# Layer 0 of a hybrid decoder step: full-size products for two small transposes, one place for a head's sample reads, and one set of four places for all merges

## The chip, the cores and the metric

The kernel runs on one core of one Trainium2 chip. The metric is the device time of one execution in microseconds: 2222.28 us is the median of three runs (2222.04 to 2224.26). A core has five engines that work side by side, each through its own instructions in order: TensorE (PE in the profile, with its weight loads as PEld), VectorE (DVE), ScalarE (ACT), GpSimd (POOL) and SyncE (SP), which here issues all DMA transfers. They wait for each other through semaphores.

## The reference: what is computed

A two-layer decoder trunk is run on a prompt of 16 + 1024 tokens and on 8 sample sequences of 8 tokens each: 1104 token columns in all, float32 throughout. Layer 0 is a gated DeltaNet, layer 1 an RWKV-7 mixer. Only layer 0 is touched by the change:

```
proj = xn @ w_in                                  # q, k, v, z, b, a
qkv, new_buf = causal_conv(qkv, conv_buf, conv_w) # width 4; new_buf = last 3 rows
L = where(strict, (k*beta) k^T * decay, 0);  A = L + I
u, wk = A^-1 [v*beta, k*beta*exp(gc)]             # unit lower triangular
step: v_new = u - wk S;  o = q_dec S + attn v_new;  S = S*exp(gl) + k_dec^T v_new
```

The causal convolution needs, for each of the 8 samples, the three rows before its first token (24 rows of history for each 128 channels), and it returns the last three rows of each of the 8 samples and of the prompt (27 rows). The triangular inverse is made of 32-row blocks: these are inverted one by one and then merged to 64 and to 128 rows. The samples' tokens read the samples' own states.

## The kernel before

**Tiling.** The 1104 columns are cut into three segments of 384, 384 and 336. A dense projection tile is 128 output channels by one segment: 24 products (8 contraction tiles, each as high x high, low x high and high x low part in a 32-bit reduced form) that add up in one PSUM buffer. In the trace these are `dq`, `dk`, `dv`, `dz`.

**Order.** Layer 0 issues its instructions in exactly the order in which they are written. `dense_gaps` emits a dense tile and calls `L.gap()` after each 6 products; this is a *gap*, and the gaps are numbered. All other work is put into the numbered gaps with `L.put(gap, function, priority)` or `L.steps`; within one gap a smaller priority comes first. A pair of value heads (j = 0 to 7) owns 72 gaps from `B = base(j) = 24 + 72 j`. So each engine's queue is a fixed sequence: an instruction that waits holds up everything behind it on its engine.

**Convolution (`conv_plan`).** For each of 32 channel tiles: `load` brings the history, 24 rows by 128 channels, from memory; `head` turns it with a PE transpose (line 607) into PSUM, from where DVE copies it into the row buffer `raw`; `out` copies a dense result into `raw`; `first` starts the taps and copies the last tokens' columns into `last` on POOL (lines 628 and 630); `ending` turns `last` (128 channels by 27 columns) with a PE transpose (line 652); `store` writes it. `hist` and `last` have two buffers each. The arithmetic helpers are `transpose` (line 126) and `mm` (line 129), so the profile shows these two lines for nearly all of PE's work.

**Preparation (`prep_plan`).** It makes the decay-weighted blocks `E`, sends their 32-row diagonal blocks through memory into `invA`, inverts them in 31 elementwise steps (lines 690 and 692; on POOL for j = 1 to 6, on DVE for j = 0 and 7), and then, in the gaps i0+1 to i0+7 after the last step's gap i0, stores the result and brings it back in two arrangements: ACT copies a turned form (line 815), which goes to memory as `g_u` (gap i0+3); `T1n` is loaded in gap i0+4 (3 transfers); `TT` for segment 0, 1 and 2 is loaded in gaps i0+5, i0+6 and i0+7 (4 transfers each), from `g_u`. SP issues them in that order, with the weight loads (`wraw`), the history loads and others in between. i0 is B+48 for j = 1 to 6.

**Merges.** `merge(s)` merges segment s in eight steps: products Y of 32 rows, their copies by DVE, products U of 32 rows (which need `TT` of segment s), their copies by ACT and DVE, Y of 64 rows, a copy, U of 64 rows, a copy. Two steps go in one gap. Segment 0 has the gaps i0+8 to i0+11, segment 1 i0+9 to i0+12, segment 2 i0+12 to i0+15. The PSUM buffers are `u` (one buffer) for segments 0 and 2, and `f` (two buffers) for segment 1. The products use only a 32x32 or 64x64 part of PE's array. A product of float32 operands shows as two records.

**Sample reads (`sample_read_plan`).** Per value head, eight products of 128 x 32 stationary columns (line 929, `usr` in the trace): four in one gap, four in the next.

**Recurrence (`recur_plan`).** Token groups of 128 follow each other every 8 gaps; their products are `rA` in the trace. They run between the same dense products.

Of the kernel before, what the change touches and what calls it, by code (L numbers as in the profile page):

```python
# [88 lines left out]
class Builder:  # L89
# [8 lines left out]
    def t(self, pool, shape, tag, bufs=1, dt=F32):  # L98
        self.uid += 1
        return pool.tile(shape, dt, name=f"{tag}_{self.uid}", tag=tag, bufs=bufs)  # L100
# [485 lines left out]
    def conv_plan(self, ends, ft, dst, done=None):  # L586

        nc, i, t, L, fp = self.nc, self.i, self.t, self.line, self.fp
        c = Ctx()
        f = slice(128 * ft, 128 * ft + 128)  # L590
        cw = [self.cw[:, k, ft:ft + 1] for k in range(4)]
        raws, ys = [], []
        wd = lambda s: SEGS[s][1] + (24 if s == 0 else 0)
        prev = lambda s: raws[s][:, wd(s):wd(s) + 3]
        v11 = lambda x: x[:, 0:88].rearrange("p (b r) -> p b r", r=11)
        v8 = lambda x: x.rearrange("p (b r) -> p b r", r=8)
        v3 = lambda x: x.rearrange("p (b r) -> p b r", r=3)

        def load():
            c.hist = t(fp, [24, 128], "hist", 2)  # L600
            nc.sync.dma_start(c.hist, i["state_gdn_conv"][0].rearrange("b r c -> (b r) c")[:, f])

        def head():
            x = t(fp, [128, 411], "raw", 3)
            raws.append(x)
            hp = self.ps("f", 2, "hist")
            self.transpose(hp[:, 0:24], c.hist)
            nc.vector.tensor_copy(v11(x)[:, :, 0:3], v3(hp[:, 0:24]))
            nc.gpsimd.memset(x[:, 88:91], 0.0)

        def out(s, p):
            n = SEGS[s][1]
            if s == 0:
                x = raws[0]
                nc.scalar.copy(v11(x)[:, :, 3:11], v8(p[:, 0:64]))
                nc.scalar.copy(x[:, 91:411], p[:, 64:384])
            else:
                x = t(fp, [128, 411], "raw", 3)
                raws.append(x)
                nc.gpsimd.tensor_copy(x[:, 0:3], prev(s - 1))  # L620
                nc.scalar.copy(x[:, 3:3 + n], p[:, 0:n])

        def first(s):
            ys.append(t(fp, [128, 408], "cvy", 2))
            self.act(ys[s][:, 0:wd(s)], raws[s][:, 0:wd(s)], AF.Identity, scale=cw[0])
            if s == 0:
                c.last = t(fp, [128, 27], "last", 2)
                nc.gpsimd.tensor_copy(v3(c.last[:, 0:24]), v11(raws[0])[:, :, 8:11])
            elif s == 2:
                nc.gpsimd.tensor_copy(c.last[:, 24:27], prev(2))  # L630

        def tap(s, *ks):
            for k in ks:
                nc.vector.scalar_tensor_tensor(ys[s][:, 0:wd(s)], raws[s][:, k:k + wd(s)], cw[k], ys[s][:, 0:wd(s)], op0=ALU.mult, op1=ALU.add)  # L634

        def tanh(s):
            self.act(raws[s][:, 0:wd(s)], ys[s][:, 0:wd(s)], AF.Tanh, scale=0.5)

        def silu(s):
            e, y, d, n = raws[s], ys[s], dst(s), SEGS[s][1]  # L640
            one = lambda d, e, y: nc.vector.scalar_tensor_tensor(d, e, 1.0, y, op0=ALU.add, op1=ALU.mult)
            if s == 0:
                one(v8(d[:, 0:64]), v11(e)[:, :, 0:8], v11(y)[:, :, 0:8])
                one(d[:, 64:384], e[:, 88:408], y[:, 88:408])
            else:
                one(d[:, 0:n], e[:, 0:n], y[:, 0:n])
                if n < 384:
                    nc.vector.memset(d[:, n:384], 0.0)

        def ending():  # L650
            lp = self.ps("f", 2, "last")
            self.transpose(lp[0:27, 0:128], c.last)
            c.ls = t(fp, [27, 128], "lasts", 1)
            nc.vector.tensor_copy(c.ls, lp[0:27, 0:128])

        def store():
            nc.sync.dma_start(self.o["s_gdn_conv"][0].rearrange("b r c -> (b r) c")[:, f], c.ls[0:24])
            nc.sync.dma_start(self.o["p_gdn_conv"][0, 0][:, f], c.ls[24:27])

        L.put(ends[0] - 11, load, 2)  # L660
        L.put(ends[0] - 2, head, 2)
        for s, e in enumerate(ends):
            L.put(e + 1, lambda s=s: first(s), 1.5)
            L.put(e + 2, lambda s=s: tap(s, 1, 2), 2)
            L.put(e + 3, lambda s=s: tap(s, 3), 2)
            L.put(e + 4, lambda s=s: tanh(s), 2)
            L.put(e + 5, lambda s=s: silu(s), 1.7)
            if done is not None:
                L.put(e + 8, lambda s=s: done(s), 2.2)
        L.put(ends[2] + 5, ending, 2.5)  # L670
        L.put(ends[2] + 8, store, 3)
        return out

# [28 lines left out]
    def gdn_front(self, right):  # L702
        self.fp = right.enter_context(self.tc.tile_pool(name="gfront", bufs=1, side="right", reuse_waits="tile"))
        self.T1n = None

    def gdn_zero(self):
        self.T1n = self.t(self.fp, [128, 18, 64], "T1n")
        self.nc.gpsimd.memset(self.T1n, 0.0)

        self.kqm = self.t(self.fp, [128, 4, 4, 32], "kqm")  # L710
        self.nc.gpsimd.memset(self.kqm, 0.0)
# [20 lines left out]
    def prep_plan(self, j, B, G, o, pace):  # L732

        nc, t, fp, col, L = self.nc, self.t, self.fp, self.col, self.line
# [97 lines left out]
        i0 = B + 15 + o + int(30 * pace)  # L832
        L.steps(i0, inv, range(1, 8), 1.4)

        v = lambda p, k: p[:, 0:6 * k].rearrange("p (c i) -> p c i", i=k)
        half = lambda s: (("u", 1), ("f", 2), ("u", 1))[s]

        def merge(s):
            LT, TT, T1 = G.E[s].rearrange("p t h k -> p (t h) k"), G.TT[s], self.T1n
# [28 lines left out]
            for q in range(6):  # L868
                self.mm(v(p, 64)[0:64, q], Ys[64:128, q], TT[64:128, q, 64:128])
            self.act(TT[0:64, :, 64:128], v(p, 64)[0:64], AF.Identity, scale=-1.0)  # L870
        for s, at in enumerate((0, 1, 4)):
            m = merge(s)
            for u in range(4):
                L.put(i0 + 8 + at + u, lambda m=m: next(m, None), 1)
                L.put(i0 + 8 + at + u, lambda m=m: next(m, None), 1.05)

    def values_done(self, G, h, s):
        nc = self.nc
# [29 lines left out]
    def sample_read_plan(self, j, B, G):  # L908

        nc, t, L = self.nc, self.t, self.line  # L910
        Sb, c = {}, Ctx()

        def load(h, g):
            x = Sb[h, g] = t(self.gp, [128, 4, 128], "Sb", 3)
            nc.sync.dma_start(x, self.i["state_gdn"][0, 4 * g:4 * g + 4, 2 * j + h].rearrange("b k v -> k b v"))

        def spread():
            kqm = self.kqm.rearrange("p b x (c r) -> p (b x c) r", r=8)
            for x, z in ((0, G.K[0]), (1, G.Q[0])):
                for g in (0, 1):  # L920
                    a = 8 * x + 4 * g
                    nc.gpsimd.tensor_copy(kqm[:, a:a + 52:17], z[:, 32 * g:32 * g + 32].rearrange("p (b r) -> p b r", r=8))

        def mults(h, bs):
            if h == 0 and bs[0] == 0:
                c.ps = self.ps("u", 1, "sr")
            for b in bs:
                for q in range(4):
                    self.mm(c.ps[32 * q:32 * q + 32, 128 * h:128 * h + 128], self.kqm[:, b, q], Sb[h, q % 2][:, b], b == 0, b == 3)

        def out():
            S = G.sS = t(self.gp, [64, 2, 256], "sS", 1)
            for x in (0, 1):
                nc.scalar.copy(S[:, x], c.ps[64 * x:64 * x + 64, 0:256])
        for g, x in ((12, (0, 0)), (14, (0, 1)), (15, (1, 0)), (22, (1, 1))):
            L.put(B + g, lambda x=x: load(*x), 3)
        L.put(B + 14, spread, 2.6)
        for g, x in ((18, (0, (0, 1))), (19, (0, (2, 3))), (26, (1, (0, 1))), (27, (1, (2, 3)))):
            L.put(B + g, lambda x=x: mults(*x), 2.5)
        L.put(B + 28, out, 2.5)  # L940

# [1690 lines left out]
```

## Time and profile before

| | |
|---|---|
| runs | 2222.28 us median of 3 (2222.04 to 2224.26) |
| the profiled execution | span 2227.4 us, 5.1 us above the runs' median |
| PE busy | 2142.1 us, 96% of the span |
| DVE, ACT, POOL busy | 1411.3, 1265.0, 1237.8 us (63, 57, 56%) |
| one group of 72 gaps of layer 0 (268.8 to 389.0) | 120.2 us, PE busy 119.2 us, POOL busy 85.4 us |
| mean granted TensorE clock | 0.977 |

The gap work of layer 0 can be followed in the trace by tile names: `fhist`, `flast`, `usr`, and `uY`, `fY`, `uU`, `fU` for the merges' products. In a timeline a row gives the start, the time from the start of its first to the end of its last instruction, the engine, the line, the operation and its tiles, and the number of instructions that follow each other; a bracket gives the idle time ahead and what ended it. The ends of pipelined products are modelled, so costs are best read from starts: the time from one dense product's start to another's, less the usual step of the dense products in between, is the price of what was put there.

### The profile page before, as it was taken

The page shows a single profiled execution, that of the slowest core. Times are in us where ns is not written, and L with a number is a line of the kernel's source. Part 1 is how long each engine was busy: PE and PEld are TensorE (multiplying, and loading weights), DVE is VectorE, ACT ScalarE, POOL GpSimd, SP SyncE. Part 2 cuts the span into 40 slices and gives each one's busy share as a digit, 9 for nine tenths or more (in the row PEclk, how much of TensorE's full clock was granted, in tenths as well). Part 3 has the DMA queues.
Part 4 walks back from the last instruction along what each step waited for, and adds up shares of the span by engine and source line. Part 5 has one row for each costly group of instructions (what it writes and reads, how often), then busy time and mean ns, then how long its engine had stood idle before and what let it go on. Part 6 is the DMA issues. An engine that isn't in the chain of part 4 may idle for free.

```text
span 2227.4 us, 55333 instructions
## 1 busy us (share of the span) xinstructions
PE 2142.1 (96%) x20382; PEld 1977.4 (89%) x20382; DVE 1411.3 (63%) x3638; ACT 1265.0 (57%) x3651; POOL 1237.8 (56%) x1890
## 2 busy tenths in 40 slices
PE   8989999999999999989999999999999999999997
PEld 7879989899999989978999999998988977888886
DVE  7858575766757585975435762667546347667764
ACT  6526565556655565645433464756546466667663
POOL 3418678585858585525241442227768646666663
PEclk9999999999999999999999999999999999999997
DMA  4324242424243333435254235587885566656532
GB/s 120 84 59 133 66 123 73 114 80 115 79 115 96 101 107 76 132 78 171 91 151 105 69 102 172 180 256 199 229 242 147 160 187 166 171 150 177 160 115 88
DMA packets 495400, 291.61 MB, mean 131 GB/s; under 512 B 222345, under 2 KB 480506, under 8 KB 495130
## 3 DMA queue, kind: packets, MB, share of 16 engines
q1 hardware_dynamic: 495130, 288.08, 46.1%
q8 instruction: 161, 2.64, 0.5%
q14 instruction: 109, 0.89, 0.1%
HBM read 195.66 MB, written 92.30 MB: 129 GB/s over the span
## 4 chain that ended last, share of the span: by engine, by line
PE 68%; DVE 13%; POOL 6%; DMA 5%; ACT 4%; issue 3%; SPq 1%; DVEq 0%; POOLq 0%; ACTq 0%
PE d L129 14%; PE dz L129 7%; PE dv L129 7%; PE rA L133 6%; PE rA L129 5%; PE zo L129 3%; PE do L129 3%; PE dk L129 3%; DVE cvy L634 2%; POOL invT L692 2%; PE fG L129 2%; POOL invtmp L690 2%; PE dq L129 2%; DMA wraw<-in_gdn_w_out 1%; DVE invT L692 1%
## 5 line engine op out<-in xcount | busy, mean ns | idle before, releaser
L143 POOL TENSOR_TENSOR wlo<-wraw,whi 128x512 fp32r<-128x512 f32 x190 | 251.4, 1324 | 229.5 <-ACT whi L139 207.2
L692 POOL TENSOR_TENSOR invT<-invT,invtmp 72x31 f32<-72x31 f32 (+36 forms) x341 | 213.4, 626 | 26.7
L634 DVE SCALAR_TENSOR_TENSOR cvy<-raw,cw,cvy 128x408 f32<-128x408 f32 (+2 forms) x288 | 203.4, 706 | 29.7 <-ACT cvy L115 25.7
L690 POOL TENSOR_TENSOR invtmp<-invA,invT 72x31 f32<-72x31 f32 (+36 forms) x341 | 202.6, 594 | 20.4 <-POOL invT L678 0.8
L129 PE MATMUL d<-xc,whi 128*128 128x384 f32 (+1 forms) x640 | 180.8, 344 | 1.0 <-ACT whi L139 0.8
L139 ACT CAST whi<-wraw 128x512 fp32r<-128x512 f32 x238 | 145.7, 614 | 27.6 <-DMA wraw<-in_rwkv_w_rkvz 13.9
L129 PE MATMUL dv<-xc,whi 128*128 128x384 f32 (+1 forms) x480 | 154.5, 343 | 0.0
L129 PE MATMUL dz<-xc,whi 128*128 128x384 f32 (+1 forms) x480 | 153.0, 342 | 0.0
L115 ACT ACTIVATE w<-rA,nbp 128x128 f32<-128x128 f32 x144 | 45.2, 364 | 152.3 <-PE rA L129 149.9
L129 PEld LDWEIGHTS d<-xc,whi 128*128 128x128 f32 x640 | 118.6, 192 | 3.5 <-ACT whi L139 1.1
L129 PE MATMUL d<-xc,wlo 128*128 128x384 f32 (+1 forms) x320 | 105.5, 339 | 1.9 <-DVE wlo L143 1.9
L160 POOL TENSOR_TENSOR ors<-ovar,cvals 128x6 f32<-128x6 f32 x24 | 34.1, 1422 | 124.6 <-DVE ovar L1122 124.6
L129 PE MATMUL dz<-xa,whi 128*128 128x384 f32 (+1 forms) x288 | 102.6, 356 | 0.5 <-DVE zg L906 0.5
L129 PE MATMUL dv<-xa,whi 128*128 128x384 f32 (+1 forms) x288 | 102.5, 356 | 0.0
L129 PE MATMUL d<-xa,whi 128*128 128x384 f32 (+1 forms) x336 | 100.1, 341 | 1.3 <-ACT whi L139 0.8
L1930 POOL TENSOR_SCALAR y<-y,mv,grs 128x64 f32<-128x64 f32 x132 | 81.7, 640 | 33.1 <-DVE grs L164 27.8
L129 PEld LDWEIGHTS dv<-xc,whi 128*128 128x128 f32 x480 | 89.3, 188 | 3.5 <-issue 3.0
L959 POOL TENSOR_SCALAR Sb<-Sb,eglb 128x128 f32<-128x128 f32 x128 | 88.8, 706 | 5.9 <-DVE usc L752 2.2
L129 PEld LDWEIGHTS dz<-xc,whi 128*128 128x128 f32 x480 | 90.4, 191 | 0.7 <-issue 0.2
L129 PE MATMUL d<-xh,whi 128*128 128x384 f32 (+1 forms) x256 | 82.3, 334 | 0.0
L129 PE MATMUL d<-xl,whi 128*128 128x384 f32 (+1 forms) x256 | 82.3, 335 | 0.0
L129 PE MATMUL d<-xh,wlo 128*128 128x384 f32 (+1 forms) x256 | 82.1, 334 | 0.0
(544 smaller groups left out, 7232.1 us busy)
## 6 DMA issues: line engine op xcount, KB each, us to landing
wraw<-in_gdn_w_in SPq DMA_DIRECT2D x96, 256.0 KB
wraw<-in_rwkv_w_rkvz SPq DMA_DIRECT2D x74, 256.0 KB
Sb<-in_state_gdn SPq DMA_DIRECT2D x64, 256.0 KB
wraw<-in_rwkv_w_o SPq DMA_DIRECT2D x48, 256.0 KB
E<-drow SPq DMA_DIRECT2D x24, 384.0 KB
attn<-drow SPq DMA_DIRECT2D x24, 384.0 KB
wraw<-in_gdn_w_out SPq DMA_DIRECT2D x36, 256.0 KB
out_s_gdn<-Sb SPq DMA_DIRECT2D x32, 256.0 KB
```

The costliest lines, as they stand in the source:

```text
L115: return self.nc.scalar.activation(out, in_, func, bias=bias, scale=scale, **kw)
L129: self.nc.tensor.matmul(out, lhsT, rhs, start=start, stop=stop)
L133: self.nc.tensor.matmul(out, lhsT, rhs, start=start, stop=True, skip_group_check=True)
L139: nc.scalar.copy(hi, x)
L143: e.tensor_tensor(lo, x, hi.bitcast(F32), op=ALU.subtract)
L160: self.nc.gpsimd.tensor_tensor(y, x, half.broadcast_to(sh), op=ALU.pow)
L634: nc.vector.scalar_tensor_tensor(ys[s][:, 0:wd(s)], raws[s][:, k:k + wd(s)], cw[k], ys[s][:, 0:wd(s)], op0=ALU.mult, op1=ALU.add)
L690: v.tensor_tensor(tmp, A[:, j, j + 1:32].unsqueeze(2).broadcast_to([nb, n, m]), Tv[:, j, 0:m].unsqueeze(1).broadcast_to([nb, n, m]), op=AL ...
L692: v.tensor_tensor(Tv[:, j + 1:32, 0:m], Tv[:, j + 1:32, 0:m], tmp, op=ALU.subtract)
L959: nc.gpsimd.tensor_scalar(Sb[g][:, u], Sb[g][:, u], self.eglb[:, hv, 4 * g + u:4 * g + u + 1], None, op0=ALU.mult)
L1930: nc.gpsimd.tensor_scalar(y[:, q], y[:, q], mv[:, q, 0:1], P.rs[:, q:q + 1], op0=ALU.subtract, op1=ALU.mult)
```

## The change

1. `hist` and `last` become one cleared buffer of 128 x 128 each, made once (`cleared`, with a POOL memset; `gdn_front` is called twice). The history's transpose becomes a full product of `hist` with the first 24 columns of the identity, the last tokens' transpose a full product of `last` with the identity. Rows or columns beyond the 24 or 27 are zero. A full product of float32 shows as two records where the transpose showed as one.
2. `ending` moves from gap e+5 at priority 2.5 to gap e+4 at priority 1.4 (e is the last segment's gap).
3. The merges of all three segments are put into the same four gaps, i0+7, i0+9, i0+11 and i0+13, two steps of each segment in each; segment 2 takes the buffers `f` in place of `u`.
4. A head's eight sample reads are put into one gap, the later of the two.

```diff
         def load():
-            c.hist = t(fp, [24, 128], "hist", 2)
-            nc.sync.dma_start(c.hist, i["state_gdn_conv"][0].rearrange("b r c -> (b r) c")[:, f])
+            c.hist = self.hist
+            nc.sync.dma_start(c.hist[0:24], i["state_gdn_conv"][0].rearrange("b r c -> (b r) c")[:, f])
...
             hp = self.ps("f", 2, "hist")
-            self.transpose(hp[:, 0:24], c.hist)
+            self.mm(hp[:, 0:24], c.hist, self.ident[:, 0:24])
...
             if s == 0:
-                c.last = t(fp, [128, 27], "last", 2)
+                c.last = self.last
...
             lp = self.ps("f", 2, "last")
-            self.transpose(lp[0:27, 0:128], c.last)
+            self.mm(lp[:, 0:128], c.last, self.ident)
...
-        L.put(ends[2] + 5, ending, 2.5)
+        L.put(ends[2] + 4, ending, 1.4)
...
     def gdn_front(self, right):
...
         self.T1n = None
+        self.hist = self.cleared("hist")
+
+    def cleared(self, tag):
+        x = self.t(self.fp, [128, 128], tag)
+        self.nc.gpsimd.memset(x, 0.0)
+        return x
 
     def gdn_zero(self):
+        self.last = self.cleared("last")
...
-        half = lambda s: (("u", 1), ("f", 2), ("u", 1))[s]
+        half = lambda s: (("u", 1), ("f", 2), ("f", 2))[s]
...
-        for s, at in enumerate((0, 1, 4)):
+        for s in range(3):
             m = merge(s)
             for u in range(4):
-                L.put(i0 + 8 + at + u, lambda m=m: next(m, None), 1)
-                L.put(i0 + 8 + at + u, lambda m=m: next(m, None), 1.05)
+                L.put(i0 + 7 + 2 * u, lambda m=m: next(m, None), 1)
+                L.put(i0 + 7 + 2 * u, lambda m=m: next(m, None), 1.05)
...
-        for g, x in ((18, (0, (0, 1))), (19, (0, (2, 3))), (26, (1, (0, 1))), (27, (1, (2, 3)))):
+        for g, x in ((19, (0, (0, 1, 2, 3))), (27, (1, (0, 1, 2, 3)))):
             L.put(B + g, lambda x=x: mults(*x), 2.5)
```

## The prediction

> **What bounds the kernel now.** I read first the page's span and busy times, then the busy times of one group of 72 gaps, then who waited for whom on PE in layer 0, and last the timelines around each operation that changes.
>
> ```profile
> span 2227.4 us, 55333 instructions
> PE 2142.1 (96%) x20382; PEld 1977.4 (89%) x20382; DVE 1411.3 (63%) x3638; ACT 1265.0 (57%) x3651; POOL 1237.8 (56%) x1890
> ```
>
> ```profile
> 268.80:389.00 120.20, 119.20 (x1028) 111.29 (x1027) 81.40 (x222) 72.21 (x233) 85.43 (x140) 1.00 0.37 98
> ```
>
> ```profile
> PE usc L129 <- DVE E L766: 3.7, 6, 0.6
> ...
> PE fU L129 <- DMA TT<-g_u: 1.3, 1, 1.3
> ```
>
> In a middle group (second block: PE, PEld, DVE, ACT, POOL, clock, DMA) PE is busy for all but 1.0 of 120.2 us; its largest wait there is the one named `usc`, once a group. So PE's own time sets layer 0: what is taken off PE is gained, and what PE waits for is lost, unless the wait is already there. The last row is a wait in which a merge's U stood for its `TT` load; it matters below. The sum is made as a difference within this execution (span 2227.4) and put on the runs' median, 2222.28, which lies 0.2% lower.
>
> **History transposes, 32.** Dense products of 384 columns start 0.175 us apart; of 336 columns, 0.155.
>
> ```profile
> 323.17 0.33 PE L129 MATMUL dv<-xc,whi 128*128 128x384 f32 x1
> 323.43 0.24 PE L126 MATMUL fhist<-ident,hist 24*128 24x24 f32 x1
> ...
> 323.88 0.34 PE L129 MATMUL dv<-xc,wlo 128*128 128x384 f32 x1
> ```
>
> From 323.17 to 323.88 are 0.71 us, less two dense steps 0.36 us: the 24-row transpose itself is short, but PE empties before it and after it the next weights load in the open. No 128-row product of 24 columns is in the trace; the nearest has 16.
>
> ```profile
> 1240.82 0.73 PE L129 MATMUL frss<-ones,rsum 128*128 128x16 f32 x6
> 1241.40 0.40 PE L129 MATMUL d<-xl,xa 128*128 128x336 f32 x1
> ```
>
> Six records take 0.58 us, about 0.1 each (bounds 0.1 and, for its quickest whole-array neighbours of 128 columns, 0.11), so a history product of two records costs 0.22: 0.14 less, times 32 = **-4.5 us** (bounds -3 and -5).
>
> **Last tokens, 32.**
>
> ```profile
> 245.91 0.34 PE L129 MATMUL dz<-xc,whi 128*128 128x384 f32 x1
> 246.09 0.27 PE L126 MATMUL flast<-ident,last 128*27 128x128 f32 x1
> ...
> 246.38 0.34 PE L129 MATMUL dz<-xa,wlo 128*128 128x384 f32 x1
> ```
>
> 0.47 less two steps is 0.12 us. The product streams 128 columns in two records: 266.92 to 267.37 below is four such records, 0.11 each, so 0.22: 0.11 more, times 32 = **+3.5 us** (bounds +3 and +4). The Trainium skill ("TensorEngine Tiling (Array Packing)", Tiling Modes) says that a change of tiling mode drains PE, and counts 128 x 32 as a mode; by it the 27-column transpose would pay about what a read pays below, and this edit would gain some 6 us instead. The 0.12 us show no such drain for this one; the history rows do show it. `ending` also comes a gap earlier. Its POOL copy of the third segment ends at 244.32 in the second value tile's turn, where POOL is behind, and PE's new place is near 244.7:
>
> ```profile
> 243.86 0.46 POOL L630 COPY last<-raw 128x3 f32<-128x3 f32 x1
> ```
>
> Elsewhere the copy has gaps to spare; I take 0 and at most 0.4 x 7 = 3 us if PE gets there sooner. `hist` with one buffer makes SP wait for the previous `head`, three gaps before the load; SP is ahead of PE only where it has no other issue for many microseconds, so 0, and some 1 us a group if that cover is gone. The clearings run on POOL before its own work begins: 0, else under 1 us.
>
> **Sample reads, 16 merged pairs.**
>
> ```profile
> 210.94 0.34 PE L129 MATMUL dv<-xa,whi 128*128 128x384 f32 x1
> 211.21 0.64 PE L129 MATMUL usr<-Sb,kqm 128*32 128x128 f32 x16
> ...
> 212.07 0.34 PE L129 MATMUL dv<-xc,wlo 128*128 128x384 f32 x1
> ```
>
> 1.13 less two steps is 0.78 us, for 16 records that follow each other in four strips at 0.11 per four = 0.44. So 0.34 us is entering and leaving the narrow mode. One of two goes: 16 x 0.34 = **-5.4 us** (bounds -4.8 and -6.4).
>
> **Merges on PE, 8 groups.**
>
> ```profile
> 268.59 0.32 PE L129 MATMUL dz<-xc,whi 128*128 128x336 f32 x1
> 268.83 0.57 PE L129 MATMUL uY<-T1n,E 32*32 32x32 f32 x24
> ...
> 269.59 0.32 PE L129 MATMUL dz<-xa,wlo 128*128 128x336 f32 x1
> ...
> 282.62 0.33 PE L129 MATMUL dk<-xa,whi 128*128 128x384 f32 x1
> 282.88 0.91 PE L129 MATMUL uY<-T1n,E 64*64 64x64 f32 x12
> ...
> 284.00 0.33 PE L129 MATMUL dk<-xc,wlo 128*128 128x384 f32 x1
> ```
>
> A Y of 32 rows costs 1.00 - 0.31 = 0.69 us, a Y of 64 rows 1.38 - 0.35 = 1.03 us. Per record they take 0.016 and 0.058 us, so 0.38 and 0.70 of that is products, and some 0.32 again entry and exit. Eight places become four: 4 x 0.32 = 1.3 us less per group; 0.3 is given back, because in the old mixed places a U and a Y of 64 rows used different parts of the array at once. 8 x -1.0 = **-8 us** (bounds -5 and -10). New places: Y32 1.46, U32 1.47, Y64 and U64 2.42 each.
>
> So PE's own work falls by 4.5 - 3.5 + 5.4 + 8.3 = 14.7 us.
>
> **What the new places wait for.** All three U of 32 rows now stand in gap i0+9; segment 2's was in i0+13. Its `TT` transfers stay in SP's gap i0+7.
>
> ```profile
> 263.62 0.31 SPq L818 DMA_DIRECT2D g_u<-invA  x1
> ...
> 266.81 1.75 SPq L828 DMA_DIRECT2D TT<-g_u  x4
> 268.66 0.40 SPq L2120 DMA_DIRECT2D wraw<-in_gdn_w_in  x1
> 269.10 3.90 SPq L828 DMA_DIRECT2D TT<-g_u  x8
> ```
>
> ```profile
> 266.92 0.61 PE L129 MATMUL rA<-X,TT 128*128 128x128 f32 x4
> 267.37 0.61 PE L129 MATMUL rA<-S,Q 128*128 128x128 f32 x4
> ...
> 271.35 0.21 PE L129 MATMUL uU<-TT,invA 32*32 32x32 f32 x1
> ```
>
> `g_u` must land (266.81) before the first `TT` goes out; twelve issues at about 0.49 us and a weight load between them end at 273.00, the last one starting at 272.55. How long one takes to land: group 0 has such waits.
>
> ```profile
> 142.20 1.76 SPq L828 DMA_DIRECT2D TT<-g_u  x4
> ...
> 144.45 1.79 SPq L828 DMA_DIRECT2D TT<-g_u  x4
> ```
>
> ```profile
> 145.41 0.22 PE L129 MATMUL uU<-TT,invA 32*32 32x32 f32 x2 [0.23 <-DMA TT<-g_u]
> ...
> 149.68 0.22 PE L129 MATMUL fU<-TT,invA 32*32 32x32 f32 x2 [1.28 <-DMA TT<-g_u]
> ```
>
> The fourth issue of segment 0 starts at 142.20 + 1.76 - 0.44 = 143.5 and PE goes on at 145.41: 1.9 us, the lower bound. That of segment 1 starts near 145.8 and PE goes on at 149.68: 3.9, the upper; the larger `g_u` took 266.81 - 263.62 = 3.2. I take 2.5, between the ends. So segment 2's U can run at 275.05. PE is there when? Gap i0+9 had its U at 271.35. The new gap i0+7 adds 1.46 - 0.69 = 0.8 us more than the old i0+8 place; U of segments 0 and 1 take 0.8; and what the group saved since its inverse began (reads 0.7, others near 0) brings PE 0.7 sooner, while POOL does not come sooner: it works without a gap to the inverse's end.
>
> ```profile
> 259.06 0.23 POOL L690 TENSOR_TENSOR invtmp<-invA,invT 72x31 f32<-72x31 f32 x1
> 259.38 0.25 POOL L692 TENSOR_TENSOR invT<-invT,invtmp 72x31 f32<-72x31 f32 x1
> ```
>
> Ready at 271.35 + 0.8 + 0.8 - 0.7 = 272.2, loaded at 275.05: PE waits 2.8 us in group 1. In group 2 the last eight issues take 1.06 us longer:
>
> ```profile
> 389.91 4.96 SPq L828 DMA_DIRECT2D TT<-g_u  x8
> ```
>
> so 3.9 there; I take 3.4 us for each of the six groups (bounds, with landings of 1.9 and 3.9, about 2 and 5): 6 x 3.4 = **+20.5 us**. Behind the waiting U stand `ktok`, the dense tile and group j-1's last state update; nothing else can run on PE. Group 0's wait of 1.28 grows to some 5 us but replaces other losses there; group 7, with fewer issues in between, should meet its loads, and two gaps between steps spare it waits on DVE: together -1 us (bounds -5 and +4). The bursts of copies (three segments at once on DVE and ACT) fit in the 1.9 us of dense work between places and the wait itself: 0, else up to 0.5 us a group.
>
> **The clock.**
>
> ```profile
> 148.30:151.70 3.40, 2.12 (x49) 1.80 (x46) 0.91 (x2) 1.27 (x4) 0.00 (x0) 1.00 0.34 65
> 151.70:155.10 3.40, 3.40 (x28) 3.18 (x25) 0.56 (x1) 0.48 (x1) 0.00 (x0) 0.51 0.62 194
> 155.10:158.50 3.40, 3.40 (x41) 2.96 (x40) 0.71 (x2) 0.82 (x2) 0.00 (x0) 0.50 0.02 5
> ```
>
> In group 0, 3.4 us in which PE stood for 1.28 and did small products for about 1 were followed by half clock for at least 6.8 us, of which PE loses half. In the groups 1 to 6 the new U place has some 1.2 us of small products and 3.4 us of wait in one stretch. I expect the clock to drop in most of them, mostly for one or two such windows of 3.4 us, with part of the first inside the wait: 2.2 us each (bounds 0 and, for three windows, 5): 6 x 2.2 = **+13 us**. The skill ("TensorE: Matmul & The Clock Gate", Part 1) lets the clock fall only after a whole idle window of about 3.4 us; by that rule nearly all these waits would cost no clock and the sum would end near 2227. The row of 148.30 speaks against it, with PE busy for 2.12 of 3.40.
>
> **Sum**: -14.7 + 20.5 - 1 + 13 = +18, so 2222.3 + 18 = **2240 us**.
>
> **Rivals.**
> 1. *The wait without the clock* (2222.3 - 14.7 + 20.5 - 1 = 2227): for it, the clock stayed at full speed in all of 268.8 to 870 in spite of the merges, and group 0's drop had more than one wait near it; against it, the wait is longer than group 0's. Chance 0.20.
> 2. *The loads are there in time* (2222.3 - 14.7 = 2207.6), the side of a gain: if `g_u` and the twelve issues came some 3 us earlier relative to PE, the edits keep what they save. It decides where the last `TT` lands before 272.2. For it: segment 0's U met its loads with over a microsecond to spare. Against it: nothing in the change moves POOL, ACT's turned copy or SP's order, and segments 1 and 2 follow at 0.49 us per issue. Chance 0.18.
> 3. *Waits and clock at their upper bounds*: 5 us and 3 us in six groups, 2222.3 - 14.7 + 30 + 18 = 2255, if landing takes 3.9 us and half clock also catches the two 64-row places (2.4 us each of small products). Chance 0.12.
>
> **How the numbers follow.** Forecast 0.50, with its own range 2230 to 2252. The range for 8 in 10 leaves out most of rival 2's middle and half of rival 3: 2210 to 2254. What this kernel can tell from no change is about 0.2%, 4.4 us. Faster: rival 2 and a little more, 0.20; same: half of rival 1, 0.11; slower: the rest, 0.69.
>
> **What would show it.** Two-record `hist` products at 0.22 us and `last` at 0.22; one `usr` row of 32 records per head; four merge places per group of 72, 36 records of 64 rows in a row; in groups 1 to 6 a wait `PE fU <- DMA TT<-g_u` of about 3 us; granted clock 0.5 behind it. No such wait would make the prediction wrong from its largest term on; waits with a clock of 1.00 would make rival 1 right.

## The result, and the profile after

The changed kernel takes **2241.44 us**, the median of five runs (2231.53 to 2245.47); the kernel before takes 2222.28 (2220.87 to 2225.82, five runs). The ratio is 1.0073, 95% interval 1.0053 to 1.0093, so the change costs 12 to 21 us. The forecast was 2240.

The page of the changed kernel (its span, then busy time of each engine):

```profile
span 2235.2 us, 55464 instructions
PE 2132.5 (95%) x20446; PEld 1989.9 (89%) x20446; DVE 1415.7 (63%) x3638; ACT 1265.0 (57%) x3651; POOL 1234.8 (55%) x1893
```

PE is busy for 9.6 us less than before, and the kernel is longer. The list of who waited for whom on PE, from 84 to 1016 us (total, times, longest), says where the time is:

```profile
PE fU L129 <- DMA TT<-g_u: 10.6, 19, 2.2
...
PE uY L129 <- DMA T1n<-g_t: 4.1, 5, 2.0
PE usc L129 <- DVE E L773: 3.7, 6, 0.6
```

The first row stood at 1.3 us in one wait; the second is new; the third is as it was. One U place of 32 rows, in group 1 (the sixth row is the next dense product):

```profile
274.18 0.61 PE L129 MATMUL rA<-w,attn 128*128 128x128 f32 x4
274.72 0.21 PE L129 MATMUL uU<-TT,invA 32*32 32x32 f32 x1
...
275.94 0.22 PE L129 MATMUL fU<-TT,invA 32*32 32x32 f32 x2 [0.36 <-DMA TT<-g_u]
...
277.13 0.18 PE L129 MATMUL fU<-TT,invA 32*32 32x32 f32 x1 [0.64 <-DMA TT<-g_u]
...
277.82 0.22 PE L129 MATMUL fU<-TT,invA 32*32 32x32 f32 x2 [0.43 <-DMA TT<-g_u]
...
278.39 0.40 PE L129 MATMUL dz<-xc,whi 128*128 128x336 f32 x1
```

```profile
266.24 0.32 SPq L825 DMA_DIRECT2D g_u<-invA  x1
...
269.38 1.76 SPq L835 DMA_DIRECT2D TT<-g_u  x4
...
271.68 4.82 SPq L835 DMA_DIRECT2D TT<-g_u  x8
```

The three U's take 3.67 us of PE, from 274.72 to 278.39. Without a wait they take 1.4 us: that step between two dense products is 2.49 us in group 2 of `e11_all_loads_early` below, where the loads are early, and 1.07 us in `e9_best_f_turn`, where no U stands in it. Segment 1 is waited for once, segment 2 twice. SP's last `TT` issue begins at about 276.1 and has landed by 277.8.

The clock behind such a place, in group 3 (stretch: length, then busy time of PE, PEld, DVE, ACT, POOL, then granted clock, DMA share, GB/s):

```profile
519.20:522.60 3.40, 2.40 (x56) 2.17 (x47) 1.04 (x4) 2.03 (x7) 0.00 (x0) 0.93 0.42 97
522.60:526.00 3.40, 3.40 (x25) 3.04 (x24) 1.11 (x5) 1.55 (x7) 0.00 (x0) 0.50 0.13 39
526.00:529.40 3.40, 3.40 (x24) 3.28 (x23) 1.93 (x5) 0.00 (x0) 0.00 (x0) 0.50 0.38 120
```

A stretch with 1.0 us of idle PE and about 1.4 us of small products is followed by 10.2 us at half clock. Over 162 to 960, where the kernel before has none, this execution has 20.4 us at half clock, in four places (3.4, 10.2, 3.4 and 3.4 us).

**Where the time went.** Groups run from one group's first `hist` product to the next one's; six of them took 719.6 us before and take 734.3 now, +14.7. What lies ahead of them is 3.3 longer and what follows, to the end of layer 0, 3.9 shorter; layer 0 ends 14.2 later. Layer 1, which nothing touched, took 1024.5 and 1018.1: two executions of the same code differ by that much. Layer 1 had some 67 us at half clock in the first and 47 in the second, which would account for it. Hence single spans (2227.4 and 2235.2) show less of the difference than the medians.

Between two such marks both kernels have exactly 432 dense products, which correspond one to one, so each start-to-start step can be compared. Means over the six groups, in us per group against the kernel before ("forecast" is the prediction's term divided by 8, for the waits and the clock by 6):

```
                          forecast    changed kernel   all loads early (below)
sample reads                -0.68        -0.75             -0.75
history products            -0.56        -0.36             -0.36
last tokens                 +0.44        +0.62             +0.59
merges, own PE time         -1.04
merges' waits               +3.4         +2.89             -0.50
half clock behind them      +2.2
all steps                   +3.8         +2.47             -1.12
```

The three merge rows are one measured figure. In "history products" only the three that stand apart from the merges are counted; the fourth stands in a merge's place and is in that row.

### The profile page after: what moved, and what is told of

It reads as the page before. It is cut to its first block, busy times and chain, and to the rows that moved or that the text cites. A ratio compares the mean times of both kernels' runs of the same rounds, so it can differ in the third digit from the quotient of the medians.

```text
span 2235.2 us, 55464 instructions
## 1 busy us (share of the span) xinstructions
PE 2132.5 (95%) x20446; PEld 1989.9 (89%) x20446; DVE 1415.7 (63%) x3638; ACT 1265.0 (57%) x3651; POOL 1234.8 (55%) x1893
## 4 chain that ended last, share of the span: by engine, by line
PE 61%; DVE 14%; DMA 7%; POOL 6%; ACT 6%; SPq 3%; issue 3%; DVEq 0%; POOLq 0%; ACTq 0%
PE d L129 11%; PE dv L129 7%; PE rA L133 6%; PE rA L129 5%; PE dz L129 5%; PE do L129 4%; PE zo L129 3%; DVE cvy L634 2%; PE dk L129 2%; POOL invT L692 2%; POOL invtmp L690 2%; PE dq L129 2%; PE fG L129 2%; SPq L835 2%; DMA wraw<-in_gdn_w_out 1%
## 5 line engine op out<-in xcount | busy, mean ns | idle before, releaser
L634 DVE SCALAR_TENSOR_TENSOR cvy<-raw,cw,cvy 128x408 f32<-128x408 f32 (+2 forms) x288 | 209.1, 726 | 45.9 <-ACT cvy L115 41.8
L690 POOL TENSOR_TENSOR invtmp<-invA,invT 72x31 f32<-72x31 f32 (+36 forms) x341 | 196.5, 576 | 21.3 <-DMA invA<-rltd 1.5
```

The source lines that it names most:

```text
L690: v.tensor_tensor(tmp, A[:, j, j + 1:32].unsqueeze(2).broadcast_to([nb, n, m]), Tv[:, j, 0:m].unsqueeze(1).broadcast_to([nb, n, m]), op=AL ...
```

## The experiments

The theory: the change shortens PE's work; what it loses are waits for loads that land after PE's new places, and the half clock behind them. The first rival: dense packets of small products cost time by themselves, through the clock and through crowded copies on DVE and ACT.

**1. Everything but the merges** (`e1_merges_as_before`): the merges go back to their places and buffers.

```diff
-        half = lambda s: (("u", 1), ("f", 2), ("f", 2))[s]
+        half = lambda s: (("u", 1), ("f", 2), ("u", 1))[s]
...
-        for s in range(3):
+        for s, at in enumerate((0, 1, 4)):
             m = merge(s)
             for u in range(4):
-                L.put(i0 + 7 + 2 * u, lambda m=m: next(m, None), 1)
+                L.put(i0 + 8 + at + u, lambda m=m: next(m, None), 1)
...
```

> The changed kernel with the merges put back to their twelve old steps and buffers; history and last-token products and the single read place stay. Theory (the loss is the wait of the merges' U for its loads, and the clock behind it): only -4.5 + 3.5 - 5.4 = -6.4 us are left, 2216 us, and the granted clock stays 1.00 from 170 to 960 us. Rival (the loss comes from the products, the single buffers or the earlier last-token step): still above 2222, up to 2235.

Measured: 2220.01 us (2213.45 to 2227.43, 12 runs) beside 2222.29; ratio 0.9987 (0.9971 to 1.0004). The time is on the theory's side of 2222 but 4 us above its 2216, and the clock did not stay at 1.00. The profiled execution, the longest of the twelve, has four stretches of 3.4 us at half clock between 170 and 960 us. Two lie in groups 2 and 4, each behind a longer wait at `usc`, where PE stood for blocks `E` that DVE, busy throughout, had not yet made. The wait from 84 to 1016 us, and the stretch before and the stretch of half clock in group 2:

```profile
PE usc L129 <- DVE E L773: 6.4, 6, 1.5
```

```profile
302.30:305.70 3.40, 1.51 (x11) 1.00 (x9) 3.40 (x9) 1.01 (x3) 3.40 (x7) 1.00 0.41 126
305.70:309.10 3.40, 3.40 (x13) 3.40 (x14) 3.33 (x8) 0.00 (x0) 1.87 (x3) 0.50 0.77 201
```

In the kernel before and in the changed one this wait is 3.7 us in six, at most 0.6; why it is longer in these two groups was not traced.

**2. The merges alone** (`e2_merges_alone`): the same lines the other way, on the kernel before.

> The kernel before with nothing changed but the merges' places and segment 2's PSUM buffer. Theory: the whole loss is here, and the 6.4 us that the other parts save are missing: 2241.4 + 6.4 = 2248 us, 2240 to 2255, with waits for the loads of 2 to 3 us per group and half clock behind most of them. Rival (the loss needs the other parts too): near 2222 or below, as PE's own merge work falls by 8 us.

Measured: 2245.51 us (2239.90 to 2249.20, 6 runs); ratio 1.0094 (1.0069 to 1.0118). Its PE waits, from 84 to 1016:

```profile
PE fU L129 <- DMA TT<-g_u: 12.8, 18, 2.4
...
PE uY L129 <- DMA T1n<-g_t: 4.9, 6, 2.0
```

All six middle groups have half clock behind the waits, 30.7 us in all. So the merge edit is the loss, all of it. The other three parts give at most a little: 2 us by the first, whose interval includes no gain at all, and 4 by the second, where the runs of the two kernels overlap. The forecast was 6.4.

**3. Later places.** Two kernels move the four places, all else as changed: to i0+9, 11, 12, 14 (`e3_merges_later`) and to i0+8, 10, 12, 14 (`e6_one_gap_later`).

```diff
-            for u in range(4):
-                L.put(i0 + 7 + 2 * u, lambda m=m: next(m, None), 1)
+            for g in (9, 11, 12, 14):
+                L.put(i0 + g, lambda m=m: next(m, None), 1)
...
```

> The changed kernel with the same grouping of the merges, but in the gaps i0+9, i0+11, i0+12 and i0+14 in place of i0+7, 9, 11, 13. Theory: U of 32 rows stands two gaps later, 3.7 to 4 us, more than the 2 to 3.2 us that it waited; the waits go, the clock stays, and PE keeps its 14.7 us: 2208 us, at most 2213 with up to 0.6 us per group of new waits where the products of 64 rows follow after one gap. Rival (72, 108 and 36 small products in a row make the clock drop or hold DVE and ACT by themselves): 2225 or more.

> The changed kernel with all merges one gap later: i0+8, i0+10, i0+12, i0+14. A gap is about 1.05 us of dense products and more with what stands in it. Theory: the wait at U of 32 rows is the last TT landing less PE's arrival, so it shrinks by the gap that PE comes later, 1.2 to 1.9 us in each of six groups, from 2.4 to under 1, and most of the half clock goes with it: 2224 (2216 to 2230), between the changed kernel (2241) and the one two to three gaps later (2225), nearer the latter. Rival (what costs is the four dense places, not the wait): 2235 or above.

Measured: `e3_merges_later` 2224.91 us (2212.58 to 2232.86, 12 runs; ratio 0.9998, 0.9979 to 1.0016); `e6_one_gap_later` 2229.56 (2217.30 to 2241.53, 12 runs; 1.0026, 1.0006 to 1.0047). The order is the theory's. The second lies in its expected range, 5 to 6 us above its 2224; the first missed, and came out where its rival stood (2225 or more). Of `e3_merges_later`, PE's waits from 162 to 960, and then from 900 to 1016:

```profile
PE fU L129 <- DMA TT<-g_u: 2.5, 5, 0.7
```

```profile
PE uY L129 <- DVE T1n L866: 6.1, 1, 6.1
```

A rest of the wait was left, and 10.2 us of half clock followed it at the end of group 6. In group 7 PE stood 6.1 us for a copy on DVE; DVE itself had stood 6.5 us for a cast on ACT, and ACT 7.0 us for the load `K<-ogd`. Groups 1 to 5 have the same small products in a row and no half clock, which speaks against its rival's cause; how much each of these losses is worth in the runs was not tried. Of `e6_one_gap_later`, one place of group 3:

```profile
516.60 0.22 PE L129 MATMUL fU<-TT,invA 32*32 32x32 f32 x2 [2.37 <-DMA TT<-g_u]
```

The expectation took a whole gap, 1.2 to 1.9 us, off the wait. By the table below PE came only 0.75 us later against the loads: 1.05 us in groups 2 and 3, less in the others and least in group 1 (0.2), where Y's place in the changed kernel had been 0.8 us longer, waiting for `T1n`, and that wait went first. The table has all kernels with merges side by side, means over groups 1 to 6, worked out from the issue of `g_u`, the landing of the last `TT` and the first U record of each group:

```
                        U in gap   last TT lands   first U    PE waits at   median of
                                   after g_u       after g_u  segment 2     the runs
e2_merges_alone          i0+9       12.0 us         8.7 us     2.5 us       2245.5
changed kernel           i0+9       11.8            8.7        2.3          2241.4
e6_one_gap_later         i0+10      12.1            9.5        1.9          2229.6
e3_merges_later          i0+11      11.7           10.3        0.7          2224.9
e7_merges_at_their_loads i0+12      12.1           11.2        0.4          2217.6
e9_best_f_turn           i0+12      11.7           11.5        0.0          2207.9
```

(The wait is the landing less the first U and 0.8 us for segments 0 and 1, where that is positive, taken group by group. The last two kernels are below.) The loads land about 12 us after `g_u` goes out, wherever the merges stand; what differs is when PE comes.

**4. The wait filled** (`e4_wait_filled`): ten full products that nothing uses, between segment 1's U and segment 2's, so that PE works while it waits.

```diff
+            if s == 2 and 0 < j < 7:
+                L.put(i0 + 9, lambda: self.busy("m", 1, 10), 1)
```

> The changed kernel with ten full 128x128x128 products of the identity, 2.2 us of PE work that nothing reads, between the U of segment 1 and of segment 2 in groups 1 to 6. Theory of the clock: the filling lies inside the wait, costs up to 0.5 us a group for entering and leaving the narrow mode, and keeps PE's activity up, so the clock stays 1.00 in most of 270 to 900 us: 2234 us, 2229 to 2238. Rival (the waits alone make the loss): 2241 to 2246.

Measured: 2238.84 us (2236.51 to 2244.26, 6 runs); ratio 1.0071 (1.0047 to 1.0095). That is 0.8 us above the expected range, and the runs overlap with the changed kernel's. In groups 1 to 6 of the profiled execution 3.4 us were at half clock, beside 20.4 in the changed kernel's and 30.7 in `e2_merges_alone`'s, which speaks for the idle PE as what lowered the clock. But the U place with its filling became 1.1 us longer by the medians of the six groups, twice what the expectation allowed, and that took back some 6 us. The table above has the cleaner proof.

**5. The loads early.** `e5_loads_early` brings `TT` in before the inverse ends, from group 0's stored blocks; `e11_all_loads_early` does so for `T1n` as well. Both leave out each later group's own blocks. PE's instructions and the places stay.

```diff
...
+        if j:
+            L.put(i0, right_back, 1.2)          # e11 only: T1n
+            for s in range(3):
+                L.put(i0 + s, lambda s=s: blocks_back(s), 1.3)
...
```

> The changed kernel, but in groups 1 to 7 the TT loads read the inverse blocks that group 0 has stored, and are issued in the gaps i0, i0+1 and i0+2, so that they wait for nothing of their own group's inverse. Left out: groups 1 to 7 merge with group 0's blocks in TT in place of their own. All instructions of PE, the places of the merges and the number of transfers stay. Theory (the waits for TT, and the half clock that follows them, are what the change loses): no wait of fU or uU for TT in groups 1 to 6, no half clock there but for a window or so, six groups of about 118 us, together 2207 (2205 to 2214, the upper part if T1n is then what Y waits for). Rival (the dense packets of small products, 24 or 36 records in a row, lower the clock and crowd DVE and ACT by themselves): groups of 121 us or more without a wait for TT, 2225 or above.

> As e5, but in groups 1 to 7 the three T1n loads, too, read what group 0 has stored, and are issued in gap i0. Left out: groups 1 to 7 merge with group 0's blocks in TT and T1n in place of their own. Theory (the change's places lose only by their loads): Y of 32 rows waits for nothing, 9.3 us less than e5's 2223.9 where these waits were on PE alone: 2215 (2211 to 2219). Rival (dense packets crowd DVE and ACT, and the wait comes back as one for a copy): 2220 or above.

Measured: `e5_loads_early` 2223.93 us (2219.75 to 2229.38, 12 runs; ratio 0.9999, 0.9985 to 1.0012), `e11_all_loads_early` **2204.62** (2201.22 to 2209.82, 6 runs; 0.9920, 0.9897 to 0.9943). The first missed its expectation because of what its own edit did on SP. Its SP queue and its PE in group 2:

```profile
384.67 2.26 SPq L812 DMA_DIRECT2D TT<-g_u  x4
387.02 0.35 SPq L834 DMA_DIRECT2D g_u<-invA  x1
387.47 1.79 SPq L837 DMA_DIRECT2D T1n<-g_t  x3
```

```profile
389.95 0.61 PE L129 MATMUL rA<-S,Q 128*128 128x128 f32 x4
390.83 0.24 PE L129 MATMUL uY<-T1n,E 32*32 32x32 f32 x2 [0.27 <-DMA T1n<-g_t]
391.33 0.53 PE L129 MATMUL uY<-T1n,E 32*32 32x32 f32 x21 [0.25 <-DMA T1n<-g_t]
```

The last four of the early `TT` issues stand right in front of `g_u` and `T1n`, so `T1n` lands when PE already stands at Y, in every group. With `T1n` early too, no U and no Y of groups 1 to 6 waits for a load and there is no half clock in them. It gains 19 us over `e5_loads_early`, twice the 9 expected; the expectation counted the waits alone, not the half clock behind them. A group of `e11_all_loads_early` and one of the changed kernel, as stretches with the columns of the windows above:

```profile
279.90:398.30 118.40, 117.32 (x1037) 112.67 (x1035) 82.52 (x222) 72.11 (x233) 84.89 (x140) 1.00 0.37 100
```

```profile
287.20:409.20 122.00, 119.72 (x1036) 114.52 (x1035) 82.66 (x222) 72.17 (x233) 84.93 (x140) 0.99 0.36 97
```

DVE and ACT have the same work in both. In this group and in group 6 they did not hold PE up at the merges, and the same 24 and 36 records in a row cost nothing beyond themselves. In groups 3 and 4 the U place is 0.9 and 0.8 us longer, and there it is a copy that PE stands for. DVE's copies of Y and the starts of the three U's in group 3:

```profile
505.92 0.73 DVE L869 COPY invA<-uY 32x192 f32<-32x192 f32 x2 [4.20 <-DMA g_u<-invA]
506.68 1.49 DVE L869 COPY invA<-fY 32x192 f32<-32x192 f32 x4
```

```profile
506.75 0.18 PE L129 MATMUL uU<-TT,invA 32*32 32x32 f32 x1
...
507.51 0.18 PE L129 MATMUL fU<-TT,invA 32*32 32x32 f32 x1 [0.18 <-PE uU L129]
...
508.26 0.18 PE L129 MATMUL fU<-TT,invA 32*32 32x32 f32 x1 [0.15 <-PE fU L129]
```

Each U starts right behind its segment's two copies, and these started late, because they write over what the store of `g_u` still reads. So the rival of the crowded copies is worth at most 0.9 us in two groups here, behind a late store; it does not make the loss. The loads' lateness, in groups 1 to 7, is worth 2241.4 - 2204.6 = 37 us (the two were timed beside 2222.28 and 2221.91), more than the forecast's 20.5 + 13.

**6. Parts that save PE time, without a new wait.** `e8_history_and_reads` is the kernel before with history products and reads in one place; `e10_reads_f_turn` turns the last tokens a gap earlier besides, as the change does. `e7_merges_at_their_loads` and `e9_best_f_turn` are these two with the merges of all segments together, in places where the loads are in; group 7 keeps its old places.

```diff
+            for g in (11, 13, 14, 15) if j == 0 else (10, 12, 13, 14) if j < 7 else range(8 + at, 12 + at):
+                L.put(i0 + g, lambda m=m: next(m, None), 1)
...
-        L.put(ends[2] + 5, ending, 2.5)         # e9 against e7, e10 against e8
+        L.put(ends[2] + 4, ending, 1.4)
```

> The kernel before with two parts of the change alone: history as a full product and a head's reads in one place; last tokens and merges as before. Theory: 4.5 + 5.5 = 10 us less PE time and no new wait: 2212 (2208 to 2217). Rival (this PE time is given back to waits for DVE and ACT, since other engines set the places): 2219 or above.

> The parts of the change that save PE time, with the merges where their loads are in: history as a full product, a head's reads in one place, the last tokens' transpose as before, the merges of all segments together in i0+10, 12, 13, 14 for groups 1 to 6 (i0+11, 13, 14, 15 in group 0), and in the old twelve places in group 7. Theory: 32 x 0.14 = 4.5 us, 16 x 0.345 = 5.5 us and 7 x 1.05 = 7.3 us less PE time and no wait of fU for TT: 2205 (2201 to 2212, the upper part if the clock drops in two or three windows). Rival (merges all together cost as much as they save wherever they stand, through the copies that crowd DVE and ACT): 2212 or above, no better than the next kernel.

> The kernel e8 (history as a full product, reads in one place; the rest as before) with the same one edit. Theory (what the two parts save was given back at the f buffer, 2.0 us over five groups, and in small waits that this edit does not touch): 2221.8 - 7 x 0.45 = 2218.5 (2214 to 2222). Rival (the order of f gives nothing): 2221 or above.

> The kernel e7 (history as a full product, reads in one place, last tokens as a transpose, merges at their loads) with one edit: the turn of the last tokens stands in gap e+4 at priority 1.4, as in the change, so the PSUM buffers f are taken in another order. In e7 the history product waits once a group 0.5 us for ACT to have read fss out of the f buffer that it takes (2.3 us over five groups). Theory: this wait goes, 7 x 0.45 = 3 us: 2214.5 (2210 to 2218). Rival (PE only waits elsewhere for the same engines): 2217 or above.

Measured: `e8_history_and_reads` 2221.82 us (2218.51 to 2232.44, 12 runs; ratio 1.0000, 0.9983 to 1.0017); `e7_merges_at_their_loads` 2217.58 (2213.12 to 2227.03, 12 runs; 0.9984, 0.9967 to 1.0000); `e10_reads_f_turn` 2219.02 (2215.13 to 2228.34, 12 runs; 0.9992, 0.9974 to 1.0010); `e9_best_f_turn` **2207.94** (2202.15 to 2215.46, 6 runs; 0.9935, 0.9910 to 0.9961).

The 10 us of the first did not come, and it and `e7_merges_at_their_loads` ended where their rivals stood. Step by step against the kernel before, a group of `e8_history_and_reads` saves 0.75 at the reads and 0.36 at two histories, and gives back 0.42 at a third, whose PE place in one group reads:

```profile
436.81 0.33 PE L129 MATMUL dv<-xc,whi 128*128 128x384 f32 x1
...
437.66 0.40 PE L129 MATMUL fhist<-ident,hist 128*128 128x24 f32 x2 [0.52 <-ACT fss L115]
437.91 0.42 PE L129 MATMUL dv<-xc,whi 128*128 128x384 f32 x1
```

PE comes sooner to a PSUM buffer `f` out of which ACT has not yet read `fss`. The same product of `e9_best_f_turn`, where `last` takes that buffer's turn earlier:

```profile
433.82 0.34 PE L129 MATMUL dv<-xc,whi 128*128 128x384 f32 x1
434.00 0.30 PE L129 MATMUL fhist<-ident,hist 128*128 128x24 f32 x2
434.13 0.42 PE L129 MATMUL dv<-xc,whi 128*128 128x384 f32 x1
```

The earlier turn is not free: it costs 0.4 us per group at `last` itself, so `e10_reads_f_turn` is only 0.5 us per group ahead of the kernel before. Merging all segments together where the loads are in takes off another 0.85 to 1.06 us (in five of six groups; nothing in the first). From `e7_merges_at_their_loads` to `e9_best_f_turn` it is 9.6 us in place of the 3 expected. Of `e7_merges_at_their_loads`, one U and the stretches around it:

```profile
626.72 0.22 PE L129 MATMUL fU<-TT,invA 32*32 32x32 f32 x2 [1.56 <-DMA TT<-g_u]
```

```profile
623.80:627.20 3.40, 1.83 (x111) 1.44 (x109) 1.50 (x6) 1.98 (x8) 0.00 (x0) 1.00 0.56 137
627.20:630.60 3.40, 3.40 (x22) 2.96 (x18) 0.85 (x2) 0.64 (x2) 0.00 (x0) 0.50 0.00 0
...
640.80:644.20 3.40, 3.40 (x14) 3.40 (x13) 0.00 (x0) 1.61 (x6) 1.62 (x3) 0.50 0.09 16
```

Its loads landed as PE arrived, in most groups; in this one 1.7 us later, and five stretches of half clock followed: this group and the next are 5.0 and 5.7 us longer than in `e9_best_f_turn`, where PE comes 0.4 us later and waits for no `TT`. That profile holds one execution; that the rest of the 9.6 us is such cases in other runs is likely but only argued.

`e9_best_f_turn` beats both kernels: 0.65% below the one before, 1.5% below the changed one.

## Why the prediction was right, point by point

**What bounds layer 0** was read rightly: PE's own time, lost one for one where it waits. `e11_all_loads_early` has the changed kernel's PE work without its waits and lands at 2204.6 (2201.2 to 2209.8); the rival "the loads are there in time" gave 2207.6. The loads were not in time, so that rival is out.

**The wait for `TT`** is there, in all six groups, at the place named, and it is the largest term. The size, 3.4 us per group, was too large: 2.3. Two steps of it failed. The landing after the last issue was 1.7 us in group 1 (about 276.1 to 277.8), and 2.0 by the mean of the six groups, not 2.5: the lower bound was nearer. And PE's own arrival, 8.6 us after `g_u` by the prediction's numbers (272.2 less 263.62), came 9.5 after it (the table's 8.7 and 0.8 for segments 0 and 1). The 0.7 us by which PE was to come sooner than POOL did not show: the inverse's last step on POOL ends 7.0 us ahead of PE's place in gap i0+7 in the changed kernel and 7.1 to 7.3 before, in every one of the six groups. POOL does not work without a gap up to there, as the prediction has it; some 40 us ahead of that place it stands 0.4 us or more for ACT's cast of a weight tile, in both kernels in each of the groups 2 to 5, so it moves along with the rest. In group 1 the new Y place in i0+7 waits for `T1n` besides (0.36 us in the row below). The prediction listed the `T1n` loads nowhere; it should have asked of each moved step what loads it needs.

```profile
269.95 0.24 PE L129 MATMUL uY<-T1n,E 32*32 32x32 f32 x2
270.55 0.53 PE L129 MATMUL uY<-T1n,E 32*32 32x32 f32 x21 [0.36 <-DMA T1n<-g_t]
```

**The clock**: 20.4 us at half clock in the six groups of the profiled execution cost PE up to 10 us, against the 13 forecast; four places in six groups, "most of them" as said. The row at 519.20 above, PE busy for 2.40 of 3.40 us, agrees with the row at 148.30 of the kernel before. The Trainium skill ("TensorE: Matmul & The Clock Gate", Part 1) names a whole idle window of about 3.4 us as what brings half clock; the clock fell here without one. Rival 1, the wait without the clock, is out: 2227 lies below all five runs. So is rival 3: 2255 lies above them.

**PE's own work.** The reads gave what was forecast (0.68 in five of six groups, 1.12 in the other). So did the merges where nothing is waited for: in `e11_all_loads_early` groups 2, 5 and 6 save 1.1 to 1.4 us, for 1.04. Its mean of 0.5 holds the late copies of groups 3 and 4 and a wait of 1.4 us of the recurrence for DVE in group 1. The median of each step over the groups, added up, is -1.12. (The prediction gives this term as -8 and takes 8.3 into its sum.) The histories were mis-sized: three of four save 0.08 to 0.14 each, and the fourth, which stands right behind narrow products, becomes 0.08 dearer, as the difference of `e8_history_and_reads` from the kernel before at that step shows. The cause is in the working of that term: the price of one isolated transpose was multiplied by 32, though one in four shares its entry and exit with a merge. The quoted 0.71 us also held part of a wait for `fss`. That is 0.28 per group in place of 0.56. The single `hist` buffer makes SP wait for the `head` before it (48 us in seven waits from 162 to 960 us), but, as forecast, at no cost to the merges: the last `TT` lands 11.8 us after `g_u`, and 12.0 in the kernel before. The last tokens cost 0.62 in place of 0.44; the gap earlier, taken at 0 with a bound of 0.4 us per group, costs about 0.4 where it is tried without the full product.

**Groups 0 and 7**, -1 us by the forecast: what lies ahead of the six groups and behind them in layer 0 came to -0.6 in the one execution, well within what the clock moves there.

**The sum** was +18 and the medians differ by 19. In the profiled execution the terms are smaller than forecast on both sides: waits 6 x 2.3 = 13.8 for 20.5, clock up to 10 for 13, PE's work about 12 less for 14.7 (8 x 0.75 for the reads, 8 x 0.28 for the histories, 8 x 1.12 for the merges, less 8 x 0.62 for the last tokens). They come to about +12; layer 0 ends 14 later there. By the runs both sides are larger: 37 us for the late loads, and 17 less than the kernel before without them (95% interval 13 to 23). What the runs have beyond the profiled executions was not traced; half clock in other places and other executions would do it. So the mechanism and its largest terms stand by experiments 2, 3 and 5, and the closeness of the total is partly luck.

## What to carry to other kernels

When work is moved together to save PE its changes of mode, list for each moved step every load it needs and place it behind the load's landing; here the same kernel took 2241 us, or 2225 with its four places up to two gaps later. PE time that is taken off shows in full only if the next engine in line has slack at the places that PE now reaches sooner: a buffer's last reader took back half a microsecond per group. A price measured on one instance in the open must not be multiplied over instances that share its cost with a neighbour.

## What the runs showed of the hardware

A wait of PE of 1.6 us was followed by 17.1 us at half clock (`e7_merges_at_their_loads`), in which PE, busy throughout, got through about half its work: of the 10.7 us that this group and the next are longer, some 9 are left beside the wait. The other four middle groups of that execution, with next to no wait there, kept full clock. Small products are not needed for it: the stretch at 302.30 of `e1_merges_as_before`, PE busy for 1.51 of 3.40 us, holds full-size products alone, and half clock followed. Nor does every such wait bring it: one of 1.4 us in group 1 of `e11_all_loads_early` did not. Half clock came in stretches of 3.4 us or multiples of it (3.4, 6.8, 10.2, 13.7, 17.1; the last stretch of each trace aside), so what a short wait costs would depend on how it and the small products around it lie against these stretches. This may be why runs of one kernel spread by 8 to 24 us, but each trace holds one execution, so it is not shown. With such a spread, differences of a few microseconds needed a dozen runs here.
